# Hybrid decoder block: raw and prepared weights in one pool of twelve tiles, a unit's weights prepared at products one to five of the unit in front

## The chip, the cores and the metric

The kernel runs on one core of one Trainium2 chip. The metric is the device time of one launch in microseconds. Three runs of the kernel before took 1889.24 to 1890.19 us, with a median of 1890.16 us.

## The reference

One layer of a decoder block over 2048 tokens of width 1024. `h` is the normalised input, `u = h @ w_in` has 8704 columns, which are split into nine parts, and two branches are made of them:

```python
h = rms_norm(x, norm_g)
u = jnp.einsum('bsd,dc->bsc', h, w_in)
v_c, b_c, c_c, z_c, q, k, v, z_a, gate_logits = jnp.split(u, SPLIT_POINTS, axis=-1)
y_c = b_c * causal_depthwise_conv(c_c * v_c, conv_w)
y_c = y_c * jax.nn.silu(z_c)
y_a = jnp.einsum('bsc,cd->bsd', y_c, w_conv_out)
...
o = sliding_window_attention(q, k, v, sinks) * jax.nn.silu(z_a)
y_b = jnp.einsum('bsc,cd->bsd', o, w_attn_out)
gates = jax.nn.sigmoid(gate_logits + gate_b)
g_a, g_b = jnp.split(gates, N_BRANCHES, axis=-1)
merged = g_a * y_a + g_b * y_b
return x + jnp.einsum('bsd,de->bse', merged, w_out)
```

All is float32. The attention has 16 query heads on 4 key heads of width 64, a window of 128 tokens and a learned sink for each head.

## The kernel before, in words

The sequence is worked in two halves of 1024 tokens (t = 0 and 1). A **unit** computes 256 output columns (two blocks of 128) for the 1024 tokens of a half (two parts of 512). Its weights are named w, then the part (q, cv, b, ga, gb, z, za, ya, yb, o), the half and the number. A cv unit takes 128 columns of C and 128 of V.

**Products.** Instead of eight products of quarter-sized blocks a unit does seven, of sums and differences of weights with sums and differences of the input (`sunit`, line 493). In time they stand in the order 1, 5, 6, 2, 7, 3, 4. When the text says "the third product of a unit" it counts in time; "product 6" is the name in the code. Each factor is kept as a high and a low float32r part; a product is four chunks times three matmuls (high x high, high x low, low x high), 12 matmuls of 128x512 (line 480). Results go to three PSUM tiles: X, V (each from a pool of two banks) and Y (one bank for all single units). Two steps of VectorE read Y in the middle of a unit:

```python
        product(Y, u, 6, ops, False)
        add(vb, s5, Y)
        ...
        product(Y, u, 7, ops, False)
        fin(1, 1, (Y, s5))
        ...
        product(Y, u, 4, ops, False)
        fin(1, 0, Y)
```

Product 7 writes Y only after `add(vb, s5, Y)` has read it (product 2 lies between), and product 4 only after `fin(1, 1, (Y, s5))` has read it (product 3 lies between). In the profile the first read is `Vcv<-s5cv,Y` and its like, the second `vr<-Y,s5cv`, `th<-Y,s5gb`, `q_t<-Y,s5q`, `b<-Y,sb`, `zs<-Y,s5z`. At the turn of the sequence's halves units run in pairs (`za2+za3`, the ya, yb and first o and ga units); then two units take turns, product by product, and the second one has a Y bank of its own.

**Weight preparation.** A unit's weights come as two raw halves of 512 KB (`load_half`, line 315), loaded by SP's queue. They are prepared in five pieces (`pieces_of`, line 353): **a** (products 1 and 2) from the first half; **d** (product 4) from the second; **sums**, four VectorE steps of 128x512 in place on the raw tiles; **s** (5 and 6); **t** (7 and 3). For a, s and t ScalarE writes the high part of 128x1024 (a cast), then VectorE the low part (the difference); for d the same in 128x512. In the profile the prepared parts are called ah, al, dh, dl or d, sh, sl, th, tl; the sums steps write `wcv_raw` and its like. s needs the sums to be done.

**Order.** The program writes the instructions tick by tick (`run`, line 687); a tick is one product. At a tick come the product and what follows on its result, then one piece (`piece`, line 435): its ScalarE half first, then up to three functions due at this tick, then its VectorE half, then the rest of the due functions; then raw loads (`ahead_loads`, line 344) and up to four small VectorE steps of chains. Due functions are the attention (64 blocks of 128 tokens and 4 heads, at hand-written ticks `AT0`, `AT1`), the finishing of units, and in the first stage the forms of the input (`OP_F`), of which form 4 is the last. Each engine works through its own list in the order written; a step that must wait holds back all behind it on its engine.

**The pools.** Before, prepared weights live in `wpool` (8 tiles of 4 KB in each partition) and raw halves in `rawpool` (4 tiles). A piece is placed when its raw halves have been issued and `live + cost` fits in 8; products give tiles back (`product`, line 471). As the eight tiles of the unit at work free up only from its third product on, the five pieces of the next unit stand at the third to the seventh product. Raw halves are loaded two units ahead, as soon as a raw tile is given back: by a unit's s and t pieces, at its sixth and seventh product.

Of the kernel before, what the change touches and what calls it, by code (L numbers as in the profile page):

```python
# [8 lines left out]
F32 = mybir.dt.float32  # L9
# [6 lines left out]
P = 128  # L16
# [3 lines left out]
H = 512  # L20
# [7 lines left out]
KP = KC // 2  # L28
# [54 lines left out]
SUM_AT = {5: 0, 6: 1, 7: 2, 4: 3}  # L83
RAW_AT = {1: (0, 0), 2: (1, 0), 3: (1, 1)}
SET_AHEAD = 3
Z_AHEAD = 2
Y_AHEAD = 4
SET_STEP = 3
# [17 lines left out]
def block_kernel(  # L106
# [17 lines left out]

    consts = ctx.enter_context(tc.tile_pool(name="consts", bufs=1))
    oppool = ctx.enter_context(tc.tile_pool(name="oppool", bufs=28))
    wpool = ctx.enter_context(tc.tile_pool(name="wpool", bufs=8))
    rawpool = ctx.enter_context(tc.tile_pool(name="rawpool", bufs=4))
    big = ctx.enter_context(tc.tile_pool(name="big", bufs=19))
    upool = ctx.enter_context(tc.tile_pool(name="upool", bufs=2))  # L130
    small = ctx.enter_context(tc.tile_pool(name="small", bufs=12))
# [6 lines left out]
    def slot(shape, dt, name):  # L138
        return big.tile(shape, dt, tag="big", name=name)
# [168 lines left out]


    plan, raws, ready, used, todo = [], {}, [], [0], []  # L310
    WRING, RAWS = 8, 4
    paired = set()
    live, rawlive = [0], [0]

    def load_half(i=None):

        if i is None:  # L320
            i = next(k for k in range(2 * len(plan)) if k not in raws)
        n, h = divmod(i, 2)
        kind, srcs, key = plan[n]
        name = "w" + "_".join(str(i) for i in key) + f"_raw{h}"
        if kind == "R":
            raw = rawpool.tile([P, 2, H], F32, tag="raw", name=name)
            for p in range(2):
                nc.sync.dma_start(raw[:, p], srcs[(2 * h + p) * P : (2 * h + p + 1) * P])

                for c in FIRST_X.get((i, p), ()):  # L330
                    xt_load(c, 0)
        else:
            raw = rawpool.tile([P, 2, KP, P], F32, tag="raw", name=name)
            w, c0 = srcs[h]
            if key[0] == "o":
                src = w[:, :, c0 : c0 + P].rearrange("(j p) r c -> r p j c", p=2)
                for p in range(2):
                    nc.sync.dma_start(raw[:, p], src[:, p])
            else:
                nc.sync.dma_start(raw, w[c0 // P].rearrange("r (p j c) -> r p j c", p=2, c=P))  # L340
        raws[i] = raw
        rawlive[0] += 1

    def ahead_loads():

        n = todo[0][0] if todo else len(ready)
        while len(raws) < min(2 * len(plan), 2 * n + 4) and rawlive[0] < RAWS:
            load_half()

    def wpair(name):  # L350
        return [wpool.tile([P, KP * UC], F32R, tag="w", name=f"{name}{i}") for i in "hl"]
# [68 lines left out]
    def open_prep():  # L420
        n = len(ready)
        if n >= len(plan):
            return False
        got = []
        for i in (n, n + 1) if n in paired else (n,):
            w, pieces = pieces_of(i)
            ready.append(w)
            got.append([(i, k) + p for k, p in enumerate(pieces)])
        if len(got) == 1:
            todo.extend(got[0])  # L430
        else:
            todo.extend(got[u][k] for u, k in PAIR_PIECES)
        return True

    def piece():

        if not todo and (len(ready) > used[0] or not open_prep()):
            return None
        n, i, cost, last, f = todo[0]
        need = [2 * n + i] if plan[n][0] == "P" else [2 * n, 2 * n + 1][: 1 + min(i, 1)]  # L440
        if live[0] + cost > WRING or any(k not in raws for k in need):
            return None
        todo.pop(0)
        live[0] += cost
        rawlive[0] -= last
        return f()

    def force(n, m):

        while m not in ready[n]:  # L450
            ab = piece()
            assert ab is not None, (plan[n], m, live)
            for f in ab:
                f()
# [217 lines left out]
        op_split(t, m, j, raw[2 * j + src[0], src[1]] if src else st["t4"][j], st["ops"])  # L672


    tick = [0]
    at = {}

    def put(n, f):
        at.setdefault(max(n, tick[0] + 1), []).append(f)
# [550 lines left out]
    def load_set(key, n0, ops):  # L1230
# [3 lines left out]
        for idx, m in enumerate(ORDER):  # L1234
            for jj in range(2):
# [24 lines left out]
                n = n0 + SET_STEP * idx + 2 + jj  # L1260
                put(n - SET_AHEAD, ld)
                for i in range(2):
                    put(n, lambda i=i, f=put_in: f(i))

    def fin_z(t, j, src, nm, key, to, at_of, eng):
# [4 lines left out]
        def load(i, q):  # L1270
            o = got[i, q] = slot([P, H], F32, f"{nm}in{t}_{j}_{i}_{q}")
            nc.sync.dma_start(o, src(2 * j + i, q))

        for (i, q), e in EVAC.items():
            put(at_of(e) - Z_AHEAD, lambda i=i, q=q: load(i, q))

# [163 lines left out]
    for t in range(NT):  # L1440
        def s(key, *srcs):
            plan.append(("S", srcs, key))

        def at_(key, c0):
            s(key, (w_in2, c0), (w_in2, c0 + P))

        if t == 0:
            for i in range(2):
                plan.append(("R", wkv[i * H : (i + 1) * H], ("kv", i)))
        for word in (SEQ0, SEQ1)[t].split():  # L1450
            both_ = word.split("+")
            for name in both_:
                if len(both_) > 1:
                    paired.add(len(plan))
                key, j = name.rstrip("0123456789"), int(name[-1]) if name[-1].isdigit() else None
                if key in ("ya", "yb"):
                    w = w_co if key == "ya" else w_ao
                    s((key, t, j), (w, j * UC), (w, j * UC + P))
                elif key == "cv":
                    s((key, t, j), (w_in2, COL_C + j * P), (w_in2, COL_V + j * P))  # L1460
                elif j is None:
                    at_((key, t), COLS[key])
                else:
                    at_((key, t, j), COLS[key] + j * UC)
                if t == 0 and name == "q0":
                    plan[-1] = ("P",) + plan[-1][1:]
    for n in range(S // P // 2):
        t, c0 = divmod(2 * n * P, T)
        if n < 2:
            paired.add(len(plan))  # L1470
        s(("o", n), (md[t], c0), (md[t], c0 + P))


# [8 lines left out]
    raw, ops, xs = st["raw"], st["ops"], st["x"]  # L1482
# [3 lines left out]
    def xt_load(c, q):  # L1486
        if c not in xts:
            xts[c] = optile(f"xt{c}", (P, T), F32)
        h = raw[c, q] = xts[c][:, hs(q)]
        nc.sync.dma_start(h, xt2[c * P : (c + 1) * P, hs(q)])  # L1490

    xt_load(0, 0)
    for n in range(4):
        load_half(n)
# [164 lines left out]
    for t in range(NT):  # L1659
# [31 lines left out]
        for word in (SEQ0, SEQ1)[t].split():  # L1691
            n = tick[0] + 1
# [74 lines left out]
```

## Time and profile before

| | |
|---|---|
| median of three runs | 1890.16 us |
| profiled execution | 1888.86 us |
| its span (first to last instruction) | 1887.1 us |
| TensorE busy | 1879.4 us, 8638 matmuls |
| VectorE busy | 1539.9 us, 2536 instructions |
| ScalarE busy | 989.2 us |
| GpSimd busy | 728.3 us |
| DMA moved | 435.81 MB, 231 GB/s in the mean |
| granted TensorE clock | 1.0 in the whole span |

A matmul's row of 0.39 us overlaps the next: from start to start a 128x512 matmul takes 0.227 us (the median of 7773). TensorE's busy share is therefore no measure of pauses below some tenths of a microsecond; its list of waits is. PE is TensorE, PEld its weight loads, DVE VectorE, ACT ScalarE, POOL GpSimd, SP the engine whose queue carries most loads. In a row of the timeline stand the start and the duration in microseconds, the engine, the line, the operation and out<-in; a bracket at the end is idle time before it and who ended it. All VectorE steps that are written through one helper have line 262, so tiles' names tell them apart. In a row of the table by stretches stand the stretch, its length, the busy time of PE, PEld, DVE, ACT and POOL with the number of instructions, the granted clock, the DMA engines' busy share and GB/s.

### The profile page before, as it was taken

The numbers are of one execution on the slowest core, as the hardware profiler recorded it, in microseconds if no ns is written. First come the engines' busy times: TensorE is split into PE (matmuls) and PEld (weight loads), VectorE is DVE, ScalarE is ACT, GpSimd is POOL, SyncE is SP. The second block draws the span as 40 slices with busy tenths as digits, with TensorE's granted clock in tenths as the row PEclk, the third lists the DMA queues.
The fourth block names the chain that finished last, engine by engine and source line by source line (L and its number), as shares of the span: only waits on it lengthen the run. The fifth ranks groups of instructions, "written<-read, shape, count | busy, mean of one in ns | idle before, by whom it ended". The sixth has DMA issues, their size and how long they took to land.

```text
span 1887.1 us, 27889 instructions
## 1 busy us (share of the span) xinstructions
PE 1879.4 (100%) x8638; PEld 1565.4 (83%) x8638; DVE 1539.9 (82%) x2536; ACT 989.2 (52%) x1993; POOL 728.3 (39%) x1038
## 2 busy tenths in 40 slices
PE   9999999999999999999999999999999999999999
PEld 7888888888888888888887888888888888888887
DVE  7989888789878889887579988988888779887654
ACT  7665554567665345435455645556566436344321
POOL 1472454556767111021075445656666211121000
PEclk9999999999999999999999999999999999999999
DMA  8475566689989978899367667768888869999653
GB/s 307 130 212 174 141 176 191 182 252 294 253 244 261 319 272 296 290 288 290 112 186 219 183 169 206 208 166 238 248 237 259 269 244 342 321 281 274 222 173 110
DMA packets 261188, 435.81 MB, mean 231 GB/s; under 512 B 33648, under 2 KB 124784, under 8 KB 261040
## 3 DMA queue, kind: packets, MB, share of 16 engines
q1 hardware_dynamic: 202848, 314.13, 50.6%
q0 software_dynamic: 58048, 119.87, 24.2%
q8 instruction: 69, 1.13, 0.3%
q14 instruction: 79, 0.65, 0.1%
q10 hardware_dynamic: 144, 0.03, 0.0%
HBM read 279.48 MB, written 154.42 MB: 230 GB/s over the span
## 4 chain that ended last, share of the span: by engine, by line
PE 84%; issue 5%; DVE 5%; DMA 3%; POOL 1%; ACT 1%; SPq 0%; POOLq 0%; DVEq 0%; ACTq 0%
PE Y L480 30%; PE Vcv L480 5%; PE Xcv L480 5%; PE s L1027 3%; PE Xz L480 2%; PE Xb L480 2%; PE Vb L480 2%; PE Vz L480 2%; PE Xza L480 2%; PE Xo L480 2%; PE Vo L480 2%; PE Vza L480 2%; PE po L1116 2%; PE Vyb L480 2%; PE Xyb L480 2%
## 5 line engine op out<-in xcount | busy, mean ns | idle before, releaser
L1078 POOL DMA_DIRECT2D x<-fd x256 | 144.2, 612 | 73.1 <-DMA fd<-f 42.9
L1099 POOL TENSOR_SCALAR_AFFINE_SELECT xh<-xh 64x512 fp32r<-64x512 f32 x64 | 67.4, 1053 | 130.2 <-DVE xl L262 95.7
L1051 ACT ACTIVATE p<-s,st,rq 128x128 f32<-128x128 f32 x256 | 113.1, 451 | 7.4 <-DMA lows<-kd 3.3
L1071 POOL DMA_DIRECT2D fd<-f x64 | 39.2, 613 | 176.3 <-DVE f L262 156.8
L480 PE MATMUL Xcv<-oph,wcv_ah 128*128 128x512 f32 x256 | 79.1, 390 | 0.0
L1132 POOL DMA_DIRECT2D od<-o x64 | 69.4, 1091 | 24.1 <-DMA od<-o 9.1
L855 POOL DMA_DIRECT2D q2d<-q_h x64 | 44.4, 693 | 82.7 <-ACT q_h L850 81.7
L1322 POOL DMA_DIRECT2D md<-thyb x32 | 27.5, 874 | 101.7 <-DVE thyb L262 88.8
L1099 POOL TENSOR_SCALAR_AFFINE_SELECT xl<-xl 64x512 fp32r<-64x512 f32 x64 | 62.5, 976 | 4.4
L1099 POOL TENSOR_SCALAR_AFFINE_SELECT yp<-xl 64x512 fp32r<-64x512 f32 x64 | 56.6, 885 | 3.1
L1099 POOL TENSOR_SCALAR_AFFINE_SELECT yp<-yp 64x512 fp32r<-64x512 f32 x64 | 54.8, 856 | 4.2
L480 PEld LDWEIGHTS Xcv<-oph,wcv_ah 128*128 128x128 f32 x256 | 47.6, 188 | 9.4
L262 DVE SCALAR_TENSOR_TENSOR y<-u,cols,y 128x512 f32<-128x512 f32 x64 | 51.5, 805 | 3.7 <-ACT y L1161 2.5
L262 DVE TENSOR_TENSOR opa<-ina,opa 128x512 fp32r<-128x512 f32 x56 | 36.2, 687 | 18.8 <-ACT opa L297 18.8
L262 DVE TENSOR_TENSOR p<-p,st 128x512 f32<-128x512 f32 x64 | 49.2, 769 | 2.8
L1051 ACT ACTIVATION_READ_ACCUMULATOR p<-s,st,rq 128x1 f32 x256 | 50.8, 198 | 0.0
L362 ACT CAST wcv_sh<-wcv_raw 128x1024 fp32r<-128x1024 f32 x16 | 16.9, 1054 | 63.9 <-DVE wcv_raw L262 63.9
L480 PE MATMUL Xcv<-oph,wcv_al 128*128 128x512 f32 x128 | 49.9, 390 | 0.0
L855 POOL DMA_DIRECT2D q2d<-q_l x64 | 44.2, 691 | 14.2 <-DVE q_l L262 10.0
L262 DVE TENSOR_TENSOR opc<-inc,opc 128x512 fp32r<-128x512 f32 x56 | 36.1, 686 | 14.4 <-ACT opc L297 14.2
L262 DVE STREAM_TRANSPOSE f<-p 128x512 f32<-128x512 f32 x64 | 45.4, 710 | 2.6 <-DVE p L262 0.2
L480 PE MATMUL Y<-oph,wcv_d 128*128 128x512 f32 x192 | 46.4, 390 | 0.0
(793 smaller groups left out, 6596.6 us busy)
## 6 DMA issues: line engine op xcount, KB each, us to landing
wcv_raw<-in_w_in SPq DMA_DIRECT2D x32, 512.0 KB, 4.1
q<-q2d SPq DMA_DIRECT2D x64, 256.0 KB, 4.7
v<-vd SPq DMA_DIRECT2D x128, 128.0 KB, 4.4
fd<-f POOLq DMA_DIRECT2D x64, 256.0 KB, 3.8
x<-fd POOLq DMA_DIRECT2D x256, 64.0 KB, 3.4
gd<-th SPq DMA_DIRECT2D x64, 256.0 KB, 3.5
wq_raw<-in_w_in SPq DMA_DIRECT2D x16, 512.0 KB, 5.1
q2d<-q_h POOLq DMA_DIRECT2D x64, 128.0 KB, 3.8
```

What stands on the lines that cost most here:

```text
L262: r = f(*args, **kw)
L362: return (lambda: nc.scalar.copy(hi, src), lambda: vec.tensor_tensor(out=lo, in0=src, in1=hi.bitcast(F32), op=ALU.subtract))
L480: nc.tensor.matmul(ps, lhsT=w[:, j, :], rhs=b[:, m, :], start=start and j == 0 and i == 0, stop=j == KP - 1 and i == 2, skip_group_check=n ...
L855: nc.gpsimd.dma_start(q2d[t][j][half, q * 2 * HB : (q + 1) * 2 * HB, i, e, :], src[HALVES[e]].bitcast(F32).rearrange("p (b x) -> p b x", x ...
L1027: nc.tensor.matmul(to, lhsT=w, rhs=x_, start=n == 0, stop=n == 2, skip_group_check=h == 1)
L1051: nc.scalar.activation(out=p[:, i, :], in_=sg[:, i, HD : 3 * HD], func=AF.Exp, bias=st[:, 1, i : i + 1], scale=rv[:, i // 2, i % 2 : i % 2 ...
L1071: nc.gpsimd.dma_start(fd, f)
L1078: nc.gpsimd.dma_start(x[QUADS[k]], src[k])
L1099: nc.gpsimd.affine_select(out=d4, in_=s4, pattern=[[0, 2], [-32 * sg, 2], [0, G], [-sg, 32]], compare_op=ALU.is_gt if prev else ALU.is_ge, ...
L1116: nc.tensor.matmul(po[:, cs], lhsT=v2[:, kind, :], rhs=xx[:, :, h * HD : (h + 1) * HD], start=h == 0 and n == 0, stop=n == 2, skip_group_c ...
L1132: put(tick[0] + ADD_WAIT, lambda: nc.gpsimd.dma_start(to, o[UH].rearrange("p c e q -> p (c e) q"), accum_op=ALU.add))
L1322: nc.gpsimd.dma_start(md[t][k, :, hs(q)], m, accum_op=ALU.add)
```

## The change

Both pools become one, `wpool`, of twelve tiles, the same memory as before. A piece is placed when prepared and raw tiles together leave room in the twelve, and only when its raw halves were issued at least three ticks before (`LANDED`). Raw halves are loaded one unit ahead of the one that is being prepared (a pair counting as one), and a first half may be loaded while the last piece of the unit in front is still to come, if there is room.

With four tiles more to use, the five pieces of a unit stand at the first to the fifth product of the unit in front (1, 5, 6, 2, 7) instead of the third to the seventh (6, 2, 7, 3, 4), two ticks earlier. Its raw halves are issued at the fourth and fifth product of the unit before that, three to four ticks ahead of their first piece, where it was ten. They take the tile that a product has just given back, so SP waits for TensorE (the end of product 2 or 3 in most units) where it waited for VectorE's s and t pieces. Among paired units the pieces move by +1 tick for the first ones and by up to 5 ticks earlier for the first unit's last piece; the raw halves of the next pair are no longer issued eight ticks before a tile is free for them. No step is added or taken away, and no length changes.

```diff
-    wpool = ctx.enter_context(tc.tile_pool(name="wpool", bufs=8))
-    rawpool = ctx.enter_context(tc.tile_pool(name="rawpool", bufs=4))
+    wpool = ctx.enter_context(tc.tile_pool(name="wpool", bufs=12))
...
-    WRING, RAWS = 8, 4
-    paired = set()
+    raw_at, tick = {}, [0]
+    WBUFS, RAWS = 12, 4
+    paired, pair_from = set(), {}
...
-            raw = rawpool.tile([P, 2, KP, P], F32, tag="raw", name=name)
+            raw = wpool.tile([P, 2, KP, P], F32, tag="w", name=name)
...
         raws[i] = raw
+        raw_at[i] = tick[0]
         rawlive[0] += 1

     def ahead_loads():

-        n = todo[0][0] if todo else len(ready)
-        while len(raws) < min(2 * len(plan), 2 * n + 4) and rawlive[0] < RAWS:
+        def behind(n):
+            n = pair_from.get(n, n)
+            return n + (2 if n in paired else 1)
+
+        n = behind(min(e[0] for e in todo) if todo else len(ready))
+        if len(todo) == 1:
+            n = behind(n)
+        while (
+                len(raws) < 2 * min(len(plan), n) and rawlive[0] < RAWS
+                and live[0] + rawlive[0] + (todo[0][2] if len(todo) == 1 else 0) < WBUFS):
             load_half()
...
-    def piece():
+    def piece(ahead=LANDED):
...
-        if live[0] + cost > WRING or any(k not in raws for k in need):
+        if live[0] + rawlive[0] + cost > WBUFS or any(
+                k not in raws or tick[0] < raw_at[k] + ahead for k in need):
             return None
```

`LANDED` is 3, and `pair_from` holds the first unit of each pair.

Two places show what moves on VectorE. The first is in unit cv 5 of the second half, behind its first read of Y and up to the second (`vr_5`, the last row); `wcv_6` is the weight of the unit behind it, and st, p, f and y are steps of the attention and of the convolution. This is the order before:

```order
L262 TENSOR_TENSOR wcv_6_al<-wcv_6_raw_11929,wcv_6_ah 128x1024
L262 SCALAR_TENSOR_TENSOR y_4_1_12189<-u_4_11933,cols,y_4_1_12189 128x512 x2
L262 TENSOR_TENSOR st_1_4_12220<-st_1_4_12220 128x4
L262 RECIPROCAL st_1_4_12220<-st_1_4_12220 128x4
L262 TENSOR_TENSOR p_1_4_12265<-p_1_4_12265,st_1_4_12220 128x512
L262 STREAM_TRANSPOSE f_1_4_12301<-p_1_4_12265 128x512
L262 TENSOR_TENSOR wcv_6_d<-wcv_6_raw_11931,wcv_6_d 128x512
L262 TENSOR_TENSOR vr_5_12319<-Y,s5cv_5_12204 128x512
```

And this is the order now, at the same place:

```order
L262 TENSOR_TENSOR wcv_6_raw_12065<-wcv_6_raw_12065,wcv_6_raw_12088 128x512
L262 SCALAR_TENSOR_TENSOR y_4_1_12186<-u_4_11926,cols,y_4_1_12186 128x512
L262 TENSOR_TENSOR wcv_6_raw_12088<-wcv_6_raw_12088 128x512
L262 SCALAR_TENSOR_TENSOR y_4_1_12186<-u_4_11926,cols,y_4_1_12186 128x512
L262 TENSOR_TENSOR wcv_6_raw_12088<-wcv_6_raw_12088,wcv_6_raw_12065 128x512
L262 TENSOR_TENSOR wcv_6_raw_12065<-wcv_6_raw_12065,wcv_6_raw_12088 128x512
L262 TENSOR_TENSOR st_1_4_12219<-st_1_4_12219 128x4
L262 RECIPROCAL st_1_4_12219<-st_1_4_12219 128x4
L262 TENSOR_TENSOR p_1_4_12262<-p_1_4_12262,st_1_4_12219 128x512
L262 STREAM_TRANSPOSE f_1_4_12302<-p_1_4_12262 128x512
L262 TENSOR_TENSOR wcv_6_sl<-wcv_6_raw_12088,wcv_6_sh 128x1024
L262 TENSOR_TENSOR vr_5_12322<-Y,s5cv_5_12201 128x512
```

The low parts of a and d (`al`, `d`) have left this stretch, and the four sums steps and the low part of s have come in; the steps of the attention and of the convolution stand as they stood.

The second place is in unit q 1 of the first half, where VectorE also makes the forms of the input: `oph_4_3` is the low part of form 4's last chunk, which product 4 of this unit needs first, and `q_1_1_1_t` is the second read of Y. This is the order before:

```order
L262 TENSOR_TENSOR k_1_0_l<-pbk_1_0_995,k_1_0_h 128x512
L262 TENSOR_REDUCE qss_0_664<-ptq_0_0_0_970 128x8
L262 TENSOR_TENSOR wq_2_d<-wq_2_raw_493,wq_2_d 128x512
L262 TENSOR_TENSOR q_1_1_1_t<-Y,s5q_1_937 128x512
L262 TENSOR_TENSOR oph_4_0_1024<-t_0_968,oph_4_0_1024 128x512
L262 TENSOR_TENSOR oph_4_1_1027<-t_1_791,oph_4_1_1027 128x512
L262 TENSOR_TENSOR oph_4_2_1030<-t_2_853,oph_4_2_1030 128x512
L262 TENSOR_TENSOR wq_2_raw_491<-wq_2_raw_491,wq_2_raw_493 128x512
L262 TENSOR_TENSOR oph_4_3_1034<-t_3_993,oph_4_3_1034 128x512
```

And this is the order now:

```order
L262 TENSOR_TENSOR wq_2_raw_831<-wq_2_raw_831,wq_2_raw_802 128x512
L262 TENSOR_TENSOR wq_2_raw_802<-wq_2_raw_802,wq_2_raw_831 128x512
L262 TENSOR_TENSOR t_3_994<-xt_176,xt_173 128x512
L262 TENSOR_TENSOR k_1_0_l<-pbk_1_0_996,k_1_0_h 128x512
L262 TENSOR_REDUCE qss_0_657<-ptq_0_0_0_967 128x8
L262 TENSOR_TENSOR wq_2_sl<-wq_2_raw_831,wq_2_sh 128x1024
L262 TENSOR_TENSOR q_1_1_1_t<-Y,s5q_1_934 128x512
L262 TENSOR_TENSOR oph_4_0_1030<-t_0_965,oph_4_0_1030 128x512
L262 TENSOR_TENSOR oph_4_1_1033<-t_1_791,oph_4_1_1033 128x512
L262 TENSOR_TENSOR oph_4_2_1036<-t_2_854,oph_4_2_1036 128x512
L262 TENSOR_TENSOR wq_2_tl<-wq_2_raw_802,wq_2_th 128x1024
L262 TENSOR_TENSOR oph_4_3_1040<-t_3_994,oph_4_3_1040 128x512
```

Of the next unit's weights, one sums step stood ahead of form 4's last chunk before; now all four sums steps, s and t do.

More of the change, by code (lines that the diff above doesn't have):

```diff
@@ L85 @@
 SET_AHEAD = 3
+LANDED = 3
 Z_AHEAD = 2
@@ L325, in load_half @@
         if kind == "R":
-            raw = rawpool.tile([P, 2, H], F32, tag="raw", name=name)
+            raw = wpool.tile([P, 2, H], F32, tag="w", name=name)
             for p in range(2):
@@ L450, in force @@
         while m not in ready[n]:
-            ab = piece()
+            ab = piece(0)
             assert ab is not None, (plan[n], m, live)
@@ L672, in form @@
         op_split(t, m, j, raw[2 * j + src[0], src[1]] if src else st["t4"][j], st["ops"])
-    tick = [0]
     at = {}
@@ L1451, in block_kernel @@
             both_ = word.split("+")
+            at0 = len(plan)
             for name in both_:
@@ L1454, in block_kernel @@
                     paired.add(len(plan))
+                    pair_from[len(plan)] = at0
                 key, j = name.rstrip("0123456789"), int(name[-1]) if name[-1].isdigit() else None
@@ L1470, in block_kernel @@
             paired.add(len(plan))
+            pair_from[len(plan)] = len(plan) - n
         s(("o", n), (md[t], c0), (md[t], c0 + P))
```

## The prediction

> **What bounds the kernel now.** I read the page's head first, then who TensorE's weight loads wait for, then VectorE's load stage by stage.
>
> ```profile
> span 1887.1 us, 27889 instructions
> ...
> PE 1879.4 (100%) x8638; PEld 1565.4 (83%) x8638; DVE 1539.9 (82%) x2536; ACT 989.2 (52%) x1993; POOL 728.3 (39%) x1038
> ```
>
> ```profile
> PEld Vq L480 <- DVE wq_sl L262: 1.1, 1, 1.1
> ...
> PEld Vv L480 <- DVE wv_sl L262: 0.8, 1, 0.8
> ...
> PEld Vq L480 <- ACT wq_sh L362: 0.7, 1, 0.7
> ...
> PEld Y L480 <- DVE zas L262: 0.6, 2, 0.3
> ...
> PEld Vcv L480 <- DVE wcv_sl L262: 0.4, 1, 0.4
> PEld Y L480 <- DVE th L262: 0.3, 1, 0.3
> ```
>
> ```profile
> 60.00:75.00 15.00, 15.00 (x68) 12.43 (x67) 15.00 (x26) 10.56 (x20) 8.57 (x13) 1.00 0.41 105
> 75.00:90.00 15.00, 14.77 (x73) 12.02 (x72) 15.00 (x24) 11.02 (x20) 8.87 (x15) 1.00 0.64 181
> ```
>
> ```profile
> 920.00:1430.00 510.00, 508.59 (x2394) 425.53 (x2393) 427.55 (x764) 293.88 (x678) 286.06 (x400) 1.00 0.71 201
> ...
> 1580.00:1740.00 160.00, 160.00 (x707) 132.51 (x706) 135.36 (x195) 71.54 (x110) 28.89 (x44) 1.00 0.93 303
> ```
>
> TensorE has work nearly all the time, so the time moves only with what it waits for. The waits that a change of weight preparation can touch are few. Four are for prepared weights: 1.1 + 0.8 + 0.7 + 0.4 = 3.0 us, all for the piece called s (names ending sh, sl). Two are for the Y bank while VectorE still reads it: 0.6 + 0.3 = 0.9 us. Nothing in the change shortens TensorE's own work. So 3.0 us, at the very most 3.9, can be gained, and the question is what new waits come. VectorE is the engine to watch: 15.00 of 15.00 us busy in the stage of the first units (third busy column), 427.55 of 510 (84%) over the second half's units.
>
> **The change, part by part.** *Weights earlier.* Every s and t piece stands two products earlier before its use. A product is 12 matmuls; a later row (12 in 2.89 us, the last one's end included) makes that about 2.7 us. Two of them, 5.4 us, are more than the longest of the four waits (1.1). All 3.0 us go: **-3.0 us**. The bounds are -3.9, when the two Y waits go too, and -1.4, when VectorE's lateness, which made s late, eats half.
>
> *What VectorE does ahead of its reads of Y.* Of a unit's pieces, a, d, sums, s and t, the middle ones now lie elsewhere against the two reads of the single Y bank. The first read is `add(vb, s5, Y)` after product 6; the second is the addition of Y and s5 in `fin(1, 1, ...)` after product 7, which must end before product 4, one product later, writes Y. Before, a and d stand between the two reads. Now four sums steps and s stand there, as the program order above shows. This is one unit of the second half, VectorE's rows and then the matmul that waits for Y:
>
> ```profile
> 1210.41 1.54 DVE L262 SCALAR_TENSOR_TENSOR y<-u,cols,y 128x512 f32<-128x512 f32 x2
> 1211.87 0.69 DVE L262 TENSOR_TENSOR Vcv<-s5cv,Y 128x512 f32<-128x512 f32 x1
> ...
> 1213.07 1.22 DVE L262 TENSOR_TENSOR wcv_al<-wcv_raw,wcv_ah 128x1024 fp32r<-128x1024 f32 x1
> 1214.20 2.37 DVE L262 SCALAR_TENSOR_TENSOR y<-u,cols,y 128x512 f32<-128x512 f32 x2
> ...
> 1219.19 0.65 DVE L262 TENSOR_TENSOR wcv_d<-wcv_raw,wcv_d 128x512 fp32r<-128x512 f32 x1
> 1219.77 0.68 DVE L262 TENSOR_TENSOR vr<-Y,s5cv 128x512 f32<-128x512 f32 x1
> 1220.37 0.68 DVE L262 TENSOR_TENSOR wcv_raw<-wcv_raw,wcv_raw 128x512 f32<-128x512 f32 x1
> ...
> 1220.88 1.32 PE L480 MATMUL Y<-oph,wcv_d 128*128 128x512 f32 x5
> ```
>
> VectorE works without a pause from the first read (1211.87) to the second, which ends at 1219.77 + 0.68 = 1220.45, only 0.43 us before product 4 starts (1220.88). The exchange of a and d for sums and s is one step of 128x1024 for another, and three more steps of 128x512. From start to start such a step takes 0.60 us (1219.77 to 1220.37), so 1.8 us more stand ahead of the second read; with the 0.69 us of a full step, 2.1. This unit falls short by 1.8 - 0.43 - 0.14 (VectorE's pauses between the reads) + 0.06 (the signal to TensorE) = 1.3 us, which TensorE must then wait.
>
> I worked the same out for the 56 single units before the output projection whose neighbours are not paired: 1.8 less the distance between the second read's end and product 4's start, less VectorE's pauses between the two reads. In 13 it is positive. Here are the tightest of them and the last in time:
>
> ```profile
> 1305.55 0.68 DVE L262 TENSOR_TENSOR th<-Y,s5gb 128x512 f32<-128x512 f32 x1
> ...
> 1306.56 1.75 PE L480 MATMUL Y<-oph,wgb_d 128*128 128x512 f32 x7
> ```
>
> ```profile
> 1393.02 0.68 DVE L262 TENSOR_TENSOR th<-Y,s5gb 128x512 f32<-128x512 f32 x1
> ...
> 1395.19 1.07 PE L480 MATMUL Y<-oph,wgb_d 128*128 128x512 f32 x4
> ```
>
> The tightest has 0.33 us, so it is 1.3 short with its pauses; the last has 1.49 us and is barely short. The 13 sum to 7.9 us. But in some of them VectorE is late already at the first read:
>
> ```profile
> 1022.20 0.39 PE L480 MATMUL Y<-oph,wcv_sl 128*128 128x512 f32 x1
> ...
> 1024.11 0.68 DVE L262 TENSOR_TENSOR Vcv<-s5cv,Y 128x512 f32<-128x512 f32 x1
> ```
>
> Product 6 has ended at 1022.59, the read starts 1.52 us later. The 1.8 us that come in between the two reads leave the stretch ahead of the first one (sums and s's low part go, those of a and d come), so here the read starts in time and the lateness pays. With each unit's lateness taken off, 9 units are short, by 5.2 us in sum: **+5.2 us**. The largest are 1.3 (1306.56), 1.3 (1220.88), 1.2 and 0.5. The bounds: with 2.1 us a unit 7.9, with 2.5, a step slowed as the y pair at 1214.20 is, 17 units and 13.7; if half of all waits come back in the next unit, 2.6.
>
> *The first units.* In the second place shown above, VectorE is never idle (the two rows of 15.00), so what is put in front of a step delays it in full. Ahead of the last low part of form 4 now stand three more sums steps, s and t of the next unit.
>
> ```profile
> 91.63 2.89 PE L480 MATMUL Y<-oph,wq_d 128*128 128x512 f32 x12
> ```
>
> ```profile
> 91.87 0.68 DVE L262 TENSOR_TENSOR oph<-t,oph 128x512 fp32r<-128x512 f32 x1
> 92.47 0.69 DVE L262 TENSOR_TENSOR wq_raw<-wq_raw 128x512 f32<-128x512 f32 x1
> 93.19 1.42 DVE L262 TENSOR_TENSOR wq_raw<-wq_raw,wq_raw 128x512 f32<-128x512 f32 x2
> ```
>
> Sums steps hang on each other and start 0.72 us apart (92.47 to 93.19); a low part of 128x1024 takes 1.13 from start to start (1213.07 to 1214.20). So 3 x 0.72 + 2 x 1.13 = 4.4 us more. The form ended at 92.55; product 4 needs it at its eleventh matmul, 91.63 + 10 x 0.227 = 93.9, so 1.35 us were to spare: **+3.0 us**, with bounds of 0 (its own inputs late anyway) and 4.4.
>
> *Loads.* A raw half is now loaded when product 2 or 3 of the unit two in front gives up a tile, three to four products (8 to 11 us) before its first use, where ten stood before.
>
> ```profile
> L340 SPq DMA_DIRECT2D wcv_raw<-in_w_in x32: 327/338/594, 96.4 to 1226.7; - x32
> ...
> DMA to landing us min/median/max: 3.1/4.1/7.4
> ```
>
> ```profile
> SPq L340 <- DVE wq_sl L262: 122.1, 6, 34.6
> ```
>
> The slowest of the 32 cv loads landed in 7.4 us, inside the 8, so I price this at 0; if SP's queue is late by 2 us more at one load in ten, ScalarE waits some 1 us each at 18 loads, and TensorE sees little of that, as ScalarE is busy 52% only: bounds 0 and +5. SP waits for these tiles in both kernels (122.1 us in six waits before, on VectorE); behind it stand the loads of attention, which it now issues no later. Where units run in pairs, Y alternates with a second bank and the Y reads have two products of time: TensorE was busy in 160.00 of 160 us there, and I price the earlier pieces at 0. The single units of the output projection have no attention beside them: 0. The first stage loads its second raw unit later, but still nine products ahead: 0.
>
> Sum: -3.0 + 5.2 + 3.0 = **+5.2 us**. The profiled execution took 1888.86 us, of which the span is 1887.1 and 1.8 lie around it; the median of the runs is 1890.16, 1.3 above. I put the difference on the median: **1895.4 us**.
>
> **A rule against, and one for.** GpSimd's selects run from 1213.28 on:
>
> ```profile
> 1213.28 1.63 POOL L1099 TENSOR_SCALAR_AFFINE_SELECT xh<-xh 64x512 fp32r<-64x512 f32 x1 [2.66 <-DVE xl L262]
> 1214.97 1.06 POOL L1099 TENSOR_SCALAR_AFFINE_SELECT yp<-yp 64x512 fp32r<-64x512 f32 x1
> ```
>
> Beside them the y pair of VectorE took 2.37 us (1214.20), ahead of them 1.54 (1210.41). The Trainium skill, SBUF — State Buffer, "SBUF: two separate sides", says that a VectorE step with two SBUF inputs and a GpSimd instruction hold one port pair in turn, whole instructions long. The trace agrees with it here; by it the sums moved into this stretch would cost like the slow pair, which is the third rival below. The Trainium skill, Perfetto Trace Analysis, "Optimization Strategy", tells to find the gaps of the engine that binds and to let what they wait for finish sooner; that is what the change does, and by it alone the sum would be -3.0 us, the first rival.
>
> **The rivals.** *Only the gain comes.* If VectorE's order bends less than I think, say because low parts of a and d that no longer stand between the reads free ScalarE's waits too, TensorE keeps its few Y waits and loses those for weights: 1890.16 - 3.0 = 1887.2, or 1886.3 with the Y waits. It is faster by 0.16 to 0.2%. For it speaks that 43 of the 56 units have the 1.8 us to spare; against it the 13 that haven't. It decides if the shortfalls come out under 0.3 us each and the first units' step costs nothing.
> *The raw halves come late.* ScalarE and VectorE then stand still in front of pieces; with the bound above 1890.16 - 3.0 + 5 = 1892.2. Against it: 7.4 us is the longest landing.
> *The port makes the moved steps longer.* At 2.5 us a unit: 1890.16 - 3.0 + 13.7 + 3.0 = 1903.9. For it: the 2.37 us pair. Against it: GpSimd is busy 286.06 of 510 us there, so not under every step.
> *The pieces do not really come earlier*, because VectorE is late all the time: then s still waits, and the gain is 1.4 instead of 3.0: 1890.16 - 1.4 + 5.2 + 3.0 = 1897.0.
>
> **How the numbers follow.** About 0.2% (3.8 us) is what a measurement of this kernel tells from no change. My forecast gets 0.42, the last rival 0.06 and the port 0.12; these are slower by more than 0.2%, but the forecast's lower part is not: if half of the waits come back, it is -3.0 + 2.6 + 3.0 = +2.6. I count 0.08 of its 0.42 as within. So slower is 0.34 + 0.06 + 0.12 = 0.52. Only the gain gets 0.33: 0.10 beyond 0.2% faster, 0.23 within. Late halves get 0.07, within. So faster 0.10, same 0.08 + 0.23 + 0.07 = 0.38, slower 0.52. The range from 1887 to 1904 leaves out the lower part of the gain at one end and the upper part of the port at the other, a tenth each. The likeliest case's own range is 1892.8 (half of the waits back) to 1898.1 (2.1 us a unit).
>
> **What would show it.** The waits for wq_sl, wv_sl, wq_sh and wcv_sl gone from TensorE's list; new ones for Y on the second read (vr, th, q_t, b), in some 9 single units between 90 and 1420 us, 0.3 to 1.5 us each; a wait of about 3 us near 92 us on form 4. I am wrong if TensorE's waits on Y stay under 2 us in sum, or if ScalarE waits for landings of raw halves.

## The result, and the profile after

The changed kernel took 1957.45 us (median of five runs, 1956.05 to 1959.82), before 1890.16 (five runs): 1.0357 times as long, interval 1.0343 to 1.0371. That is 67.3 us slower; 5.2 were forecast, and the range ended at 1904. The profiled execution has a span of 1954.7 us, 67.6 more than before.

The head of the changed kernel's page, busy times per engine:

```profile
span 1954.7 us, 27838 instructions
...
PE 1898.7 (97%) x8638; PEld 1570.3 (80%) x8638; DVE 1546.0 (79%) x2536; ACT 986.2 (50%) x1993; POOL 733.0 (37%) x1038
```

Every engine ran as many steps as before, and VectorE worked hardly longer (1546.0 us, before 1539.9). TensorE stood still. Its weight loads' list of waits (us in total, times, longest):

```profile
PEld Y L491 <- DVE vr L262: 14.5, 10, 2.7
PEld Y L491 <- DVE q_t L262: 11.8, 5, 4.2
PEld Y L491 <- DVE th L262: 11.4, 7, 3.6
PEld Y L491 <- DVE b L262: 4.5, 4, 2.0
PEld Y L491 <- DVE Vq L262: 3.5, 3, 2.5
PEld Y L491 <- DVE Vcv L262: 3.1, 2, 1.8
PEld Y L491 <- DVE Vz L262: 2.8, 3, 1.8
PEld Y L491 <- DVE zs L262: 2.0, 1, 2.0
```

No wait for wq_sl, wv_sl, wq_sh or wcv_sl is left: the forecast gain is there. In its place come waits for Y, of two kinds: `vr`, `q_t`, `th`, `b` and `zs` are the second read, `Vq`, `Vcv` and `Vz` the first. The table by stretches for two of the stretches that the prediction showed (columns as there; the same times hold a little other work now, as all is later, 2273 matmuls in the first row where it was 2394):

```profile
920.00:1430.00 510.00, 493.52 (x2273) 409.57 (x2272) 406.88 (x718) 270.73 (x602) 246.17 (x343) 0.99 0.64 185
1580.00:1740.00 160.00, 160.00 (x707) 132.28 (x706) 138.60 (x199) 78.28 (x122) 25.81 (x48) 1.00 0.85 305
```

Among the single units of the second half TensorE is now busy 493.52 of 510 us (before 508.59), among pairs still 160 of 160. The clock there is 0.99, where it was 1.00 throughout.

I then took every matmul's start in both traces and subtracted the usual distance to the next one (0.227 us for 128x512). What is left over, in us, with the number of places, adds up to the whole difference (three of the eleven "other waits" after, 0.36 us each, are no waits but wide distances right behind the three longest pauses, and belong to the row above them):

| | before | after |
|---|---|---|
| product 4 waits for the second read of Y (over 0.3 us) | 0 | 39.9 (23) |
| product 7 waits for the first read of Y (over 0.3 us) | 0 | 9.5 (8) |
| matmuls that start 0.427 instead of 0.227 us apart (below) | 0 | 7.2 (36) |
| other waits over 0.3 us | 3.5 (6) | 8.6 (11) |
| distances below 0.3 us | 2.9 | 8.9 |
| the first 7 us of the kernel | 2.7 | 2.5 |
| sum | 9.1 | 76.7 |

The unit that the prediction took as its example, VectorE's rows from the first read to the second, and then the matmul that waits:

```profile
1263.83 0.69 DVE L262 TENSOR_TENSOR Vcv<-s5cv,Y 128x512 f32<-128x512 f32 x1
...
1265.03 0.68 DVE L262 TENSOR_TENSOR wcv_raw<-wcv_raw,wcv_raw 128x512 f32<-128x512 f32 x1
...
1266.79 1.21 DVE L262 TENSOR_TENSOR wcv_raw<-wcv_raw 128x512 f32<-128x512 f32 x1
...
1269.05 1.96 DVE L262 TENSOR_TENSOR wcv_raw<-wcv_raw,wcv_raw 128x512 f32<-128x512 f32 x2
...
1272.68 1.18 DVE L262 TENSOR_TENSOR wcv_sl<-wcv_raw,wcv_sh 128x1024 fp32r<-128x1024 f32 x1
1273.79 0.68 DVE L262 TENSOR_TENSOR vr<-Y,s5cv 128x512 f32<-128x512 f32 x1
```

```profile
1274.52 0.73 PE L491 MATMUL Y<-oph,wcv_d 128*128 128x512 f32 x2 [2.08 <-DVE vr L262]
```

GpSimd's select beside the sums step at 1266.79:

```profile
1266.40 1.06 POOL L1109 TENSOR_SCALAR_AFFINE_SELECT yp<-yp 64x512 fp32r<-64x512 f32 x1
```

The four sums steps and the low part of s stand between the reads, as the order said. Product 4 waited 2.1 us; 1.3 were forecast. From the end of the first read to the end of the second it took 9.95 us (1274.47 less 1264.52), before 7.89 (1220.45 less 1212.56): 2.06 more, not 1.8.

### The profile page after: what moved, and what is told of

Its sections match the earlier page's. It is cut to its first block, busy times and chain, and to the rows that moved or that the text cites. A ratio compares the mean times of both kernels' runs of the same rounds, so it can differ in the third digit from the quotient of the medians.

```text
span 1954.7 us, 27838 instructions
## 1 busy us (share of the span) xinstructions
PE 1898.7 (97%) x8638; PEld 1570.3 (80%) x8638; DVE 1546.0 (79%) x2536; ACT 986.2 (50%) x1993; POOL 733.0 (37%) x1038
## 4 chain that ended last, share of the span: by engine, by line
PE 59%; DVE 15%; issue 10%; DMA 7%; POOL 4%; ACT 4%; SPq 1%; DVEq 0%; POOLq 0%; ACTq 0%
PE Y L491 21%; PE Xcv L491 3%; PE Vo L491 2%; PE Xo L491 2%; PE Vyb L491 2%; PE Xyb L491 2%; PE Vcv L491 2%; PE Xga L491 2%; PE Yyb L491 2%; PE Vya L491 2%; PE Xya L491 2%; PE Xb L491 2%; PE Vga L491 2%; PE Yya L491 1%; PE Vb L491 1%
## 5 line engine op out<-in xcount | busy, mean ns | idle before, releaser
L1109 POOL TENSOR_SCALAR_AFFINE_SELECT yp<-yp 64x512 fp32r<-64x512 f32 x64 | 59.9, 936 | 6.5 <-ACT yp L1096 2.4
L1109 POOL TENSOR_SCALAR_AFFINE_SELECT yp<-xl 64x512 fp32r<-64x512 f32 x64 | 61.0, 952 | 3.1
L262 DVE TENSOR_TENSOR xl<-x,xh 128x512 fp32r<-128x512 f32 x64 | 43.7, 682 | 17.9 <-DMA x<-fd 5.4
L491 PEld LDWEIGHTS Y<-oph,wcv_d 128*128 128x128 f32 x192 | 35.2, 188 | 21.5 <-DVE vr L262 14.5
L1058 ACT ACTIVATE st<-st 128x4 f32<-128x4 f32 x64 | 13.1, 205 | 76.9 <-DVE st L262 76.7
```

The source lines that it names most:

```text
L262: r = f(*args, **kw)
L491: nc.tensor.matmul(ps, lhsT=w[:, j, :], rhs=b[:, m, :], start=start and j == 0 and i == 0, stop=j == KP - 1 and i == 2, skip_group_check=n ...
L1058: nc.scalar.activation(out=st[:, 3], in_=st[:, 2], func=AF.Exp)
L1109: nc.gpsimd.affine_select(out=d4, in_=s4, pattern=[[0, 2], [-32 * sg, 2], [0, G], [-sg, 32]], compare_op=ALU.is_gt if prev else ALU.is_ge, ...
```

## The experiments

Places of a single unit's pieces at the products of the unit in front, in time, and when its raw halves are issued there (in the unit before that). "First" and "second" are TensorE's waits of over 0.3 us for the two reads, counted as in the table above; the median is beside that of the kernel before on the same chip (1889.1 to 1890.2).

| kernel | a | d | sums | s | t | raw halves | first, us | second, us | median, us | ratio, interval |
|---|---|---|---|---|---|---|---|---|---|---|
| before | 3 | 4 | 5 | 6 | 7 | two units ahead | 0 | 0 | 1890.2 | |
| changed | 1 | 2 | 3 | 4 | 5 | 4, 5 | 9.5 | 39.9 | 1957.5 | 1.0357, 1.0343 to 1.0371 |
| first | 3 | 4 | 5 | 6 | 7 | 6, 6 | 1.6 | 0 | 1904.0 | 1.007, 1.0053 to 1.0087 |
| second | 1 | 2 | 5 | 6 | 7 | 5, 5 | 14.0 | 0.6 | 1908.5 | 1.0094, 1.0079 to 1.011 |
| third | 1 | 2 | 3 | 6 | 7 | 4, 4 | 10.8 | 10.5 | 1915.3 | 1.0131, 1.0116 to 1.0146 |
| fourth | 2 | 3 | 4 | 5 | 6 | 5, 6 | 8.6 | 29.3 | 1938.5 | 1.0256, 1.024 to 1.0271 |
| fifth (changed, s's low part behind the second read) | 1 | 2 | 3 | 4 | 5 | 4, 5 | 12.2 | 14.9 | 1927.8 | 1.0198, 1.0181 to 1.0214 |
| sixth (second, low parts of a, d behind the first read) | 1 | 2 | 5 | 6 | 7 | 5, 5 | 4.2 | 2.2 | 1904.2 | 1.0071, 1.0054 to 1.0088 |
| seventh | 3 | 4 | 5 | 6 | 7 | 4, 4 | 0 | 2.5 | 1893.5 | 1.0019, 1.0009 to 1.0028 |
| eighth (seventh, v and q1 earlier) | 3 | 4 | 5 | 6 | 7 | 4, 4 | 0 | 5.7 | 1901.6 | 1.0065, 1.0051 to 1.0079 |
| ninth | 3 | 4 | 5 | 6 | 7 | 3, 3 | 0 | 0 | 1893.4 | 1.0023, 1.0014 to 1.0033 |

**First: the old places with the new pool.** A piece waits until the unit in front has started so many products; the rest is as changed.

```diff
+HOLD = (3, 4, 5, 6, 7)
...
         n, i, cost, last, f = todo[0]
+        u = used[0] - 1
+        if (ahead and n == u + 1 and plan[n][0] == plan[u][0] == "S" and not {n, u} & paired
+                and len(done.get(u, ())) < HOLD[i]):
+            return None
```

> The changed kernel with its pool of twelve and its late loads, but a single unit's pieces held back to the third to seventh product of the unit in front, where they stood before. Theory B (work on VectorE between the two reads of Y: a and d before, 1.7 us; four sums steps and s now, 3.5 us): the time goes back to 1887 to 1893 us. Theory A (pieces in the first two products, which were free of them, stand ahead of attention's steps on ScalarE and VectorE and ahead of the first read): the same, 1887 to 1893. Theory L (raw halves issued three to four ticks ahead of use, and SP waiting for TensorE with attention's loads behind it): still over 1930.

1903.95 us, outside all three forecasts. So 53.5 of the 67.3 us come from where the pieces of single units stand (the raw halves, which follow them, are issued one or two ticks later too), and 13.8 remain, which neither A nor B foresaw and which is far less than L said. Part of it is seen in ScalarE's list of waits for landings of raw halves in single units, part in one wait of TensorE:

```profile
ACT wgb_ah L373 <- DMA wgb_raw<-in_w_in: 5.3, 3, 3.5
ACT wga_ah L373 <- DMA wga_raw<-in_w_in: 3.6, 2, 2.1
ACT wz_ah L373 <- DMA wz_raw<-in_w_in: 2.8, 2, 1.9
ACT wcv_ah L373 <- DMA wcv_raw<-in_w_in: 1.7, 1, 1.7
```

```profile
1182.91 0.59 PE L1042 MATMUL s<-lows,kq 128*128 128x384 f32 x1 [3.46 <-ACT p L1066]
```

ScalarE waited 13.4 us for raw halves, before 2.4 (one time). The eight halves that ended these waits were issued only 3.7 to 6.7 us before ScalarE wanted them, and landed 5.7 to 9.2 us after their issue. The wait of TensorE at 1182.91 is for exponentials, and these stood behind a store, as ScalarE's row there shows:

```profile
1180.99 0.46 ACT L1066 ACTIVATE p<-s,st,rq 128x128 f32<-128x128 f32 x1 [6.83 <-DMA od<-o]
```

That store isn't a raw half. GpSimd issued it at 1171.76, between the two raw halves of a cv unit (1171.50 and 1171.97), and it landed at 1180.97, 9.2 us later; the 64 stores of its kind take 5.1 us in the median:

```profile
1171.50 0.93 SPq L342 DMA_DIRECT2D wcv_raw<-in_w_in  x2
```

```profile
1171.76 1.10 POOL L1147 DMA_DIRECT2D od<-o  x1
```

**Second: only a and d early.** Besides the numbers, raw halves may be issued when two pieces are still to come, so that a can stand at the first product.

```diff
+HOLD = (1, 2, 5, 6, 7)
...
-        if len(todo) == 1:
+        if 0 < len(todo) <= 2:
             n = behind(n)
```

> The changed kernel with only pieces a and d early (first and second product); sums, s and t at the fifth, sixth and seventh product as before. No piece's work stands between the two reads of Y. Theory B: 1886 to 1891 us, no waits for Y. Theory A: 1925 to 1957, since a and d stand ahead of attention in the first two products as in the changed kernel. Theory L: over 1930, as raw halves are issued three ticks ahead of use.

1908.53 us, 4.6 over the first, and outside all three forecasts: far below A and L, but not where B put it. Theory B said there would be no waits for Y. There is one of 0.6 us on the second read, but 14.0 us in eleven units on the first. One of them, VectorE's rows, and then product 7:

```profile
165.57 1.22 DVE L263 TENSOR_TENSOR wcv_al<-wcv_raw,wcv_ah 128x1024 fp32r<-128x1024 f32 x1
...
167.50 0.16 DVE L263 TENSOR_TENSOR st<-st 128x4 f32<-128x4 f32 x1 [0.70 <-ACT p L1066]
...
170.69 0.68 DVE L263 TENSOR_TENSOR wcv_d<-wcv_raw,wcv_d 128x512 fp32r<-128x512 f32 x1
171.29 0.69 DVE L263 TENSOR_TENSOR Vcv<-s5cv,Y 128x512 f32<-128x512 f32 x1
```

```profile
172.03 0.73 PE L496 MATMUL Y<-oph,wcv_th 128*128 128x512 f32 x2 [1.25 <-DVE Vcv L263]
```

The low parts of a and d now stand in front of the first read, and VectorE has one pause of 0.70 us between `wcv_al` and it. In 37 of 59 single units (the prediction's 56, k and two za) the first read comes over 0.3 us later than before, 0.84 us in the mean of all.

**Third: a, d and sums early.** The second with other numbers.

```diff
-HOLD = (1, 2, 5, 6, 7)
+HOLD = (1, 2, 3, 6, 7)
```

> The changed kernel with pieces a, d and sums at the first, second and third product, as changed, and s and t at the sixth and seventh as before. Between the two reads of Y stand four sums steps, 2.4 us, where before it were 1.7 us and in the changed kernel 3.5 us. Theory B: by proportion (0.7 of 1.8 us of added work, so 0.4 of 67 us) 1900 to 1920 us. Theory A: 1930 to 1957.

1915.31 us, where theory B put it. The work between the reads grew by 0.96 us in the mean, and 12 units wait for the second read, 10.5 us in sum.

**Fourth: one product earlier.** The first with other numbers.

```diff
-HOLD = (3, 4, 5, 6, 7)
+HOLD = (2, 3, 4, 5, 6)
```

> The changed kernel with pieces at the second to sixth product: one product earlier than before, one later than changed. Between the two reads of Y stand d and four sums steps, 3.0 us. Theory B: by proportion (1.3 of 1.8 us) 1925 to 1945 us. Theory A: one piece in the first two products where the changed kernel has two: 1905 to 1930. Theory L: as the changed kernel, over 1940.

1938.54 us, inside B's range, outside A's and 1.5 us under L's, which the second experiment had put out already. VectorE has 1.70 us more work between the reads, and 22 units wait 29.3 us for the second one.

**Fifth: the low part of s behind the second read.** The VectorE half of s is kept for one product; ScalarE's half stays.

```diff
+            held.append(lo)
+            return hi, None
...
+            while held and True:
+                held.pop(0)()
             hi, lo = (piece() if tick[0] >= W_FROM else None) or (None, None)
```

> The changed kernel with one VectorE step moved: the low part of s of single units stands behind the second read of Y (one product later), its ScalarE half stays. Between the reads remain the four sums steps. Theory B (what counts is the work on VectorE between the reads, and the low part of s, 1.1 us, brings most units over their spare): 1910 to 1922 us, near the third experiment's 1915. Rival (ScalarE, which stands at the high part of s until the sums are done, holds up attention behind it): over 1940.

1927.81 us: this one step, about 1.1 us long, is worth 29.6 us of the changed kernel's time. The second read's waits fall from 39.9 to 14.9 us. It isn't as low as B said (1910 to 1922): the first read's waits are 12.2 us, and 3.2 us go to half rate. The rival, over 1940, is out.

**Sixth: the low parts of a and d behind the first read.** The same edit on the second experiment, for a and d, released at the third product.

```diff
+HELD = (0, 1)
...
+            while held and len(done.get(used[0] - 1, ())) >= 3:
+                held.pop(0)()
```

> The second experiment (only a and d early) with the low parts of a and d on VectorE moved behind the first read of Y, where they stood before; their ScalarE halves stay in the first two products. Theory V (the low parts on VectorE make the first read late): the waits for the first read (14 us there) fall under 4 us, 1895 to 1901 us. Theory S (the casts on ScalarE ahead of attention's exponentials make it late): they stay over 10 us, 1905 to 1910.

1904.24 us, between the two forecasts. The first read's waits fell from 14.0 to 4.2 us, in four units: nearly as theory V said, so VectorE's low parts were most of that lateness. The time fell only by 4.3 us, less than V said, since other waits grew (from 5.2 to 12.0 us): in the weight loads' list wq_sl stands with 1.9 us (0.7 in the second), wcv_sl with 1.6 (0.6), and a copy of X on ScalarE with 2.2 (0.2).

**Seventh: raw halves two products earlier.** The first, with loads allowed while three pieces are still to come.

```diff
-        if len(todo) == 1:
+        if 0 < len(todo) <= 3:
             n = behind(n)
```

> The first experiment (old ticks) with the raw halves of single units issued two products earlier, at the fourth product instead of the sixth of the unit before. If the late raw halves make the 13.8 us that the first experiment keeps over before: 1890 to 1896 us, without its wait of 3.6 us at 1179. If they don't: 1901 to 1906.

1893.51 us. Of the 13.8 us that the first experiment kept, 10.4 go with the time at which the raw halves are issued. That is two things which the runs don't part: the late halves themselves, and transfers of attention that shared their time, such as the store behind the wait at 1182.91, which is gone too. (The edit also puts later pieces of the pairs back to where they stood before; the two waits at ya there fell by 0.8 us.) ScalarE no longer waits for any raw half of a single unit, though the loads take nearly as long (cv's, issue to landing, minimum, median and maximum in the first and in the seventh, 4.1 in the median before):

```profile
DMA to landing us min/median/max: 3.5/5.8/9.4
```

```profile
DMA to landing us min/median/max: 3.6/5.2/9.0
```

**Eighth: earlier where VectorE has room.**

```diff
+EARLY = {("v", 1): 2, ("q", 1, 1): 1}
...
-                and len(done.get(u, ())) < HOLD[i]):
+                and len(done.get(u, ())) < HOLD[i] - (EARLY.get(plan[n][2], 0))):
```

> The seventh experiment (old ticks, raw halves at the fourth product) with the weights of units v and q1 of the second half alone prepared earlier, by two products and by one: there VectorE has much idle time, no attention runs, and TensorE waited for pieces of s (0.6 and 1.3 us at 959 and 999). If earlier pieces pay where VectorE has room: these two waits go, 1891 to 1892.5 us, level with before. If they bring new waits for Y there: 1893.5 or more.

1901.58 us, 8 us slower than the seventh. The wait at 959 is gone, but a new one of 3.9 us stands at 953, again for the second read, and the one behind it, at 1006, grew from 0.9 to 2.1 us. VectorE's rows between the reads there:

```profile
946.22 0.69 DVE L264 TENSOR_TENSOR wv_raw<-wv_raw,wv_raw 128x512 f32<-128x512 f32 x1
...
949.71 0.75 DVE L264 SCALAR_TENSOR_TENSOR q_l<-q_t,gqk,q_h 128x512 fp32r<-128x512 f32 x1 [1.86 <-ACT q_h L866]
...
953.12 0.65 DVE L264 TENSOR_TENSOR wv_raw<-wv_raw 128x512 f32<-128x512 f32 x1
...
956.75 0.68 DVE L264 TENSOR_TENSOR q_t<-Y,s5q 128x512 f32<-128x512 f32 x1
```

The sums steps share their place with a chain of small steps (the norms of k, from 946.82 to 952.99) and with `q_l`, for which VectorE stands still 1.86 us. Idle time in the mean of a stage is no room between two given steps.

**Ninth: raw halves three products earlier.** As the seventh, with four pieces still to come.

```diff
-        if 0 < len(todo) <= 3:
+        if 0 < len(todo) <= 4:
             n = behind(n)
```

> The seventh experiment with raw halves another product earlier (third product). If the lead of the loads still counts: 1890 to 1892 us. If four more ticks were enough: 1893 to 1895, as the seventh.

1893.40 us: no further gain. The 4 us over before that are left are mostly the first units (a wait of 1.8 us at 79, before 0.5) and the pairs (1.1 and 1.4 us at 733 and 761, before 0.4 and 0.7), and waits of this kind stand there in the other kernels with the new pool too. None of them beat the kernel before.

**Tenth: the price of a late read by itself.** On the kernel before, in the output projection.

```diff
+EXTRA = {2: 4, 3: 6, 4: 7, 5: 8, 6: 9, 7: 11}
...
         product(Y, u, 7, ops, False)
+        if key[0] == "o" and u not in paired:
+            junk = slot([P, H], F32, f"junk{nm}")
+            for _ in range(EXTRA[key[1]]):
+                add(junk, s5, Y)
         fin(1, 1, (Y, s5))
```

> The kernel before with added VectorE steps of 128x512 (a throwaway sum of Y and s5) in front of the second read of Y in the six single units of the output projection, 4, 6, 7, 8, 9 and 11 of them: no attention runs there, and the read has 1.83 us to spare. At 0.6 us a step TensorE waits 0.6, 1.8, 2.4, 3.0, 3.6 and 4.8 us, 16 us in sum: 1905 to 1907 us if a wait costs its length alone. If a long wait is followed by matmuls at half rate, as after the waits of 3.3 us and more in the changed kernel, it is 2 to 10 us more.

1920.7 us, 31.6 over before (ratio 1.0166, 1.0153 to 1.018), above both forecasts. The steps were dearer than the 0.6 us that I took: they hang on each other and start 0.72 us apart, so the distances lost at the six waits are 1.0, 2.4, 3.2, 3.9, 4.6 and 6.0 us, 21.1 in sum. Another 8.4 us are matmuls at half rate. TensorE's rows behind the first three waits, twelve matmuls each, with the pause ahead of them in brackets:

```profile
1786.18 3.04 PE L481 MATMUL Y<-opw,wo_d 128*128 128x512 f32 x12 [0.82 <-DVE o L263]
...
1807.81 4.61 PE L481 MATMUL Y<-opw,wo_d 128*128 128x512 f32 x12 [2.28 <-DVE o L263]
...
1831.77 4.62 PE L481 MATMUL Y<-opw,wo_d 128*128 128x512 f32 x12 [3.00 <-DVE o L263]
```

After a pause of 0.82 us the twelve take 3.04 us, after 2.28 us 4.61. So a long wait costs more than its length, here 1.4 to 2.2 us more.

Put in a row, the medians split the 67.3 us: time of issue of the raw halves and the changed places in pairs and first units 13.8 (the first experiment; 10.4 of it the time of issue), a and d early 4.6 (the second), sums early 6.8 (the third), ScalarE's half of s and all of t early 12.5 (the fifth, in which the raw halves are later too), the low part of s between the reads 29.6.

The row holds in this order only. ScalarE waits for raw halves of single units 13.4 us in the first, 7.9 in the second, 3.2 in the third and 4.2 in the changed kernel, so the 10.4 of the first experiment are not 10.4 of the changed kernel's 67.3, and 4.6 and 6.8 are what a, d and sums cost less what the halves got better. Against the seventh, in which ScalarE has no such wait, the third is 21.8 us slower and not 11.4, and the changed kernel 63.9. So the places of the pieces are worth 53.5 to 63.9 us. The one large term that doesn't hang on the order is the last: the fifth experiment differs from the changed kernel in one step's place.

## Why the prediction was wrong, step by step

**Weights earlier, -3.0.** Right: all four waits are gone.

**The reads of Y, +5.2.** The place was right, the size was not: 39.9 us on the second read and 9.5 on the first. The nine units that were counted as short all waited, but for some 17 us in sum and not 5.2 (the two of 1.3 waited 1.8 and 2.2, at gb 1 and cv 5 of the second half); another fourteen waited as well. From each unit's spare before and what changed in it, the sum of shortfalls can be built up again. These figures are estimates from the two traces, and move by some us with the choice of units and of what counts as a pause. It is 5.2 as forecast; 7.9 without the relief at the first read; 21.8 if VectorE's pauses between the reads shrink only as they really did, instead of being used up in full; 28.8 with the work that really came in, 2.16 us in the mean instead of 1.8; 42.7 with the first read as late as it really was. So three steps failed.

- "Here the read starts in time and the lateness pays": it was the reverse. I compared how much work stands between the second read of a unit and the first read of the next, and it did shrink, but the low parts of a and d now stand right in front of the first read, which in 29 of 59 units came over 0.3 us later, 0.53 in the mean. The second and sixth experiments show these low parts to be most of the cause where a and d alone are early; for the changed kernel itself that is carried over and not run. Some 14 us here, and the 9.5 at product 7, which the forecast did not have at all.
- Pauses of VectorE are not all to be had: the forecast took off each unit's pauses in full, as if VectorE could fill them, but what ends a pause can move too, and new ones come. In `gb0` of the second half a new one of 2.5 us came up, which the profile puts down to a transfer that landed 5.6 us after its issue (why it came when it did is not shown), and TensorE then lost 3.3 us:

```profile
1452.36 0.69 DVE L262 TENSOR_TENSOR xl<-x,xh 128x512 fp32r<-128x512 f32 x1 [2.50 <-DMA lows<-kd]
```

- 1.8 us a unit was the lower of the two values that I had. Measured are 2.16, just over the upper one (2.1); a sums step grew to 1.21 us beside one of GpSimd's selects (1266.79 and 1266.40 above; 0.68 at 1265.03). So the port rival looks like a part of the truth, which no run tests by itself; but 2.5 us a unit was too much, and its sum, built with the same two errors, was too small.

The spares lie close together: in 28 of 59 units the second read ended 1.8 to 2.7 us before product 4's start. With that it fits that 0.96 us more work (the third experiment) costs 10.5 us in 12 units and 2.16 costs 39.9 in 23.

**The first units, +3.0.** Form 4 itself cost 0.8 us (a wait at 96); other places of that stage lost 1.5 at 75 and 1.2 at 92. The size was about right, the place only in part, so the size is in part luck (the 1.2 at 92 is a wait for the second read of Y, and stands in the 39.9 above too).

**Loads, 0, with a bound of +5.** Wrong in the first experiment, where the time of issue was worth 10.4 us; in the changed kernel itself ScalarE waited 4.2 us for raw halves of single units, and what that cost TensorE is not measured. Two steps of it failed. I held the longest landing of the 32 cv loads (7.4 us) for the longest of all, but in the trace of before 12 of the 132 halves of single units took over 8 us. For gb's loads the same view of before says:

```profile
DMA to landing us min/median/max: 3.2/4.9/10.0
```

And the lead was not 8 to 11 us: the halves that came late were issued 3.7 to 6.7 us before ScalarE wanted them in the first experiment, 4.2 to 7.4 in the changed kernel. A late raw half then holds up all of ScalarE's list behind it, exponentials too.

**Pairs, 0.** Nearly right: TensorE is busy 160 of 160 us, and the two waits at ya in the first half grew from 1.1 to 2.5 us in sum.

**Not in the sum at all:** half rate after long waits, 7.2 us (8.3 with the three wide distances), and 6.0 more in distances below 0.3 us, most of them 0.11 us right behind a wait.

**The rivals.** Only the gain: no. The pieces not earlier: no, they were. Late halves: they came, but beside the waits for Y, not in place of them; in the first experiment their time of issue cost twice the bound, in the changed kernel their share is not measured. The port: see above.

## What to carry to other kernels

Where a step on one engine moves, write down for every place that must be met the work that stands right in front of it, before and after, not the total of the stretch; and count a pause as room only if what ends it stays where it is. A list of spares says more than a sum at one value: if many lie just above the value that you take, a few tenths more bring a multiple. A load's lead runs from its issue to the moment its reader wants it, not from tick to tick, and has to be held against the landings of all loads of its kind; what the loads do to transfers that share their new time, the trace of before does not show.

## What the runs showed of the hardware

A wait of TensorE can cost more than its length. In the changed kernel four waits, of 2.2 to 3.9 us, are followed by 6 to 11 matmuls of 128x512 that start 0.427 us apart, not 0.227, 1.2 to 2.2 us each time. This is the longest such stretch, twelve matmuls in 5.49 us:

```profile
481.63 5.49 PE L491 MATMUL Y<-oph,wgb_d 128*128 128x512 f32 x12 [3.31 <-DVE th L262]
```

In the tenth experiment, the profile's granted clock falls behind such a wait to 0.91 in the mean of 20 us:

```profile
1800.00:1820.00 20.00, 17.72 (x72) 14.17 (x71) 12.86 (x18) 4.10 (x5) 0.00 (x0) 0.91 0.38 124
```

The Trainium skill, TensorE: Matmul & The Clock Gate, "What's actually happening", says that the array's clock drops to half after an idle window of about 3.4 us. The traces agree with the halving but not with the length. In the traces of all twelve kernels, behind the first 8 us, every one of the 11 pauses of 3.1 us and more was followed by it, none below 2.1 us was, and of the 16 between 2.1 and 3.1 us five were (2.1 to 2.4 us: once in the changed kernel, once each in the second, third, fifth and tenth experiments), while one of 3.05 us in the changed kernel (at 141) and two of 2.95 in the fourth experiment were not. What decides between them stays open.
